# Attention in two query groups, the first pair of tiles routed during the second; one tile's activations gathered and led through the gates into the dense v

## The chip, the cores and the metric

The kernel runs on one core of one Trainium2 chip. The metric is the device time of one execution in microseconds (us). The kernel before takes 4099.25 us, the median of two runs (4098.07 and 4100.43). "TensorE" is the matrix engine (PE in the rows, PEld its weight loads), VectorE is DVE, ScalarE is ACT, GpSimd is POOL, and SP issues most of the DMAs.

## The reference, cut to what matters

Two layers over 512 latent and 256 context tokens. Layer 0 mixes with a state-space scan, layer 1 with attention (8 heads, keys for all 768 tokens, queries for the 512 latent ones). Each is followed by PEER: every token picks, in each of 8 heads, 16 of 16384 experts, and sums the experts' rows:

```python
idx, gate = peer_route(t, w_q, keys)             # 128 experts for each token
act = gelu(einsum('td,tkd->tk', h, u_tab[idx])) * gate
out = einsum('tk,tkd->td', act, v_tab[idx])
```

In layer 1 only the latent tokens are left: four tiles of 128 tokens, numbered 2 to 5.

## The kernel before, in words

A tile's PEER can be computed in two ways. **Gathered:** GpSimd fetches, by an indirect DMA, for each of 128 picks one u row for each token (a tile `row`, 128x1024 f32, 512 KB), VectorE multiplies it with the tile's input and sums it into one column of `act`; after gelu and the gate, 128 v rows are gathered and added up on VectorE (`gather`, lines 1323, 1330 and 1335). Five such `row` buffers exist, which wq and some attention tiles share. **Dense:** TensorE multiplies all 16384 u rows, in 128 blocks, with the dense tiles' inputs `Hs` (`dense_u`, line 1111: 24 matmuls a block, for the high and low halves of the operands), gelu gives `ge`, which is multiplied with a dense matrix of gates `Gt`, split into A's halves, and multiplied with the blocks of v (line 1180: 18 matmuls of 512 columns a block for three tiles). The gate matrix of a tile is made out of its routing by `gate_matrix`: 16 steps of 8 tokens, one-hot rows `e` and `o` on VectorE and ScalarE, small products `g_ps` on TensorE, and a copy to HBM (`gm`), from where `Gt` is read once per 8 blocks.

Layer 1 before: tiles 4, 2 and 3 are dense, tile 5 is gathered. `mla` runs attention over all 512 queries, head by head: `project` makes a head's queries and keys (`qps`, `kp_mla`), `scores` does a head's scores for one tile of queries, `values` the product with v; VectorE takes maxima and normalizes in each of these 32 steps. When attention is done come the output product and LayerNorm of both pairs of tiles (`out_steps`, line 791), the modulation and the routing queries (`query_steps`, line 920), then the routing of each tile (`route`, a long row of small VectorE operations). While tiles are routed, `ahead` computes 48 of the 128 u blocks early and puts them into HBM (`ged`), and `gate_matrices` follows the routed tiles. `peer` runs the rest: `dense_held` goes through the 128 blocks (80 of them with u still to do) with the sums held in PSUM, and the gather of tile 5 beside it.

The order on each engine comes from `merge`: it draws steps from several streams, always from the one whose clock (the sum of the numbers that its steps yield) is least; streams under `side` may be left unfinished. An engine executes its instructions in the order that results. `peer` first merges the gate matrices and the early u blocks, with the gather as a side stream, and only then the held pass.

Of the kernel before, what the change touches and what calls it, by code (L numbers as in the profile page):

```python
# [21 lines left out]
KD = 8  # L22
# [23 lines left out]
KU, LH, KL, GQ = 2, 4, 2, 4  # L46
GA = 3
# [60 lines left out]
class Net:  # L108
# [28 lines left out]
    def spare(self, shape, name, dt=F32):  # L137
        return self.pool.tile(shape, dt, tag="spare", bufs=max(3, len(self.tiles)), name=name)
# [673 lines left out]
    def s5_layer(self, dense, gather):  # L812
# [39 lines left out]
        def memory_ctx(_):  # L852
# [5 lines left out]
                                        self.query_steps(0, (2, 3), lambda: self.Hall[:, :, :, 0:256]),  # L858
                                        self.query_steps(0, (4, 5), lambda: self.Hall[:, :, :, 256:512]))
# [12 lines left out]
    def peer_setup(self, l, dense, gather):  # L872
        self.keysT = self.t4([128, 8, 128], "keysT")
        self.load(self.keysT, self.a["peer_keysT"][l])
        self.tiles, self.gathered = dense, gather
        self.h1 = {}
        self.qT, self.m, self.gat, self.routed = {}, {}, {}, {}
        self.gm = self.dram.tile([16, 128, len(dense), 4, 8, 32], F32, name=f"gm{l}")

    def peer_memory(self, l):  # L880
        self.phase(f"peer{l}")
        self.Hall = self.big([128, 2, KD, T_LAT], "Hs", F32R)
        self.Hs = self.Hall[:, :, :, T_LAT - len(self.tiles) * 128:]

    def query_steps(self, l, pair, H):
# [7 lines left out]
        def modulate(i, ti):  # L893
            mT = st[i] = self.mod_transpose(self.h1[pair][i], l, s, 3)
            if ti in self.tiles:
# [36 lines left out]
    def route(self, ti):  # L932
# [3 lines left out]
        dense = ti in self.tiles  # L936
# [90 lines left out]
        V.scalar_tensor_tensor(out=idx, in0=ii[:, 0, :], scalar=128.0, in1=ii[:, 1, :], op0=ALU.mult, op1=ALU.add)  # L1027
        gk = self.c5([128, 128], "gk")
# [57 lines left out]
    def gate_matrices(self, n_tiles):  # L1086
# [15 lines left out]
    def dense_u(self, Us):  # L1102

        PE, S = self.nc.tensor, self.nc.scalar
        TD = len(self.tiles) * 128
# [11 lines left out]
    def ahead(self, l, blocks, n_tiles):  # L1117

        NT = len(self.tiles)
# [15 lines left out]
    def dense_held(self, l):  # L1135
# [4 lines left out]
        NT = len(self.tiles)  # L1140
        TD = NT * 128
# [8 lines left out]
        def prep_u(b):  # L1150
# [4 lines left out]
            if b in self.early:  # L1155
                ge = self.t2([128, TD], "ge")
# [4 lines left out]
        def work_u(b, x):  # L1161
            ge = x if b in self.early else self.dense_u(x)
            gv = ge.rearrange("p (d g t) -> p d g t", d=NT, g=4)
            V.tensor_tensor(out=gv, in0=gv, in1=Gt[b // SB][:, :, :, b % SB, :], op=ALU.mult)
# [143 lines left out]
    def gather(self, l, row_time):  # L1308
# [3 lines left out]
        for ti in self.gathered:  # L1312
# [77 lines left out]
    def mla(self, dense, gather):  # L1390
# [73 lines left out]
        W = self.big([128, 12288], "mla_w")  # L1464
        wuq = W[:, 0:4608].rearrange("p (k n) -> p k n", k=3)
        wuqs = W[:, 4608:6144].rearrange("p (k n) -> p k n", k=3)
        wukv = W[:, 6144:10240].rearrange("p (k n) -> p k n", k=2)
        cosT, sinT = W[:, 10240:10752], W[:, 10752:11264]
# [3 lines left out]
        for k in range(2):  # L1472
            self.load(wukv[:, k, :], a["mla_w_ukv"][k * 128:(k + 1) * 128, :])
# [3 lines left out]
        wv = wukv.rearrange("p k (h x d) -> p k h x d", h=8, x=2)  # L1477
        for ti in range(6):
            for hf in range(2):
                vp = self.ps([128, 4, 128], "vp")  # L1480
                for k in range(2):
                    PE.matmul(out=vp, lhsT=ckvT[k][:, ti * 128:(ti + 1) * 128], rhs=wv[:, k, hf * 4:(hf + 1) * 4, 1, :],
                              start=(k == 0), stop=(k == 1))
                S.copy(out=v[ti][:, hf * 512:(hf + 1) * 512].rearrange("p (h d) -> p h d", h=4), in_=vp)
        oT, heads = [], {}

        def project(h):
            if h % 2 == 0:
                oT.append(self.t4([128, 2, T_LAT], "oT"))
                rp, rs = self.ps([128, 512], "rp"), self.ps([128, 512], "rs")  # L1490
                for k in range(3):
                    PE.matmul(out=rp, lhsT=wuq[:, k, 1024 + h * 64:1024 + (h + 2) * 64], rhs=cqT[k], start=(k == 0), stop=(k == 2))
                for k in range(3):
                    PE.matmul(out=rs, lhsT=wuqs[:, k, h * 64:(h + 2) * 64], rhs=cqT[k], start=(k == 0), stop=(k == 2))
                qr, qt = self.t2([128, T_LAT], "qr"), self.t2([128, T_LAT], "qt")
                V.tensor_tensor(out=qr, in0=rp, in1=cosT, op=ALU.mult)
                V.tensor_tensor(out=qt, in0=rs, in1=sinT, op=ALU.mult)
                V.tensor_tensor(out=qr, in0=qr, in1=qt, op=ALU.add)

                qs = self.row([128, 2, T_LAT], "qs", F32R)  # L1500
                for x in range(2):
                    r, o = slice(64 * x, 64 * x + 64), slice(64 - 64 * x, 128 - 64 * x)
                    S.copy(out=qs[r, x], in_=qr[r])
                    V.tensor_tensor(out=qs[o, x], in0=qr[r], in1=qs[r, x].bitcast(F32), op=ALU.subtract)
            else:
                qs = heads[h - 1][1]
            qnT = self.row([128, 2, T_LAT], "qnT", F32R)
            qps = self.ps([128, 512], "qps")
            for k in range(3):
                PE.matmul(out=qps, lhsT=wuq[:, k, h * 128:(h + 1) * 128], rhs=cqT[k], start=(k == 0), stop=(k == 2))  # L1510
            self.split(qnT[:, 0], qnT[:, 1], qps, V)
            kn = [self.t4([128, T], "knT", F32R) for _ in range(2)]
            for c0, n in ((0, 512), (512, 256)):
                kp = self.ps([128, 512], "kp_mla")
                for k in range(2):
                    PE.matmul(out=kp[:, 0:n], lhsT=wukv[:, k, h * 256:h * 256 + 128], rhs=ckvT[k][:, c0:c0 + n],
                              start=(k == 0), stop=(k == 1))
# [149 lines left out]
```

## Time and profile before

| | |
|---|---|
| median of the runs | 4099.25 us |
| the profiled execution | 4107.66 us, span of its instructions 4105.9 us |
| TensorE busy, mean granted clock | 91% of the span, 0.956 |
| VectorE, ScalarE, GpSimd busy | 75%, 35%, 30% |
| line 1111 (dense u), both layers | 1187.4 us with the high half of u, 759.6 us with the low half |
| DMA | 986 MB, 240 GB/s over the span |

Layer 1 begins at about 2334 us. Its attention runs from 2470 to 2686 us, the output product and the queries to 2806, routing with early u blocks to about 2955, gate matrices to 3182, the held pass from 3207 to 4087, and the last LayerNorms to 4106. A row of a window gives each engine's busy time in that stretch with the number of its instructions in brackets, then the granted clock, the share of the DMA engines' time and GB/s. In a timeline a row has start, length, engine, line and what is written and read; starts of successive matmuls lie closer than their lengths, since they are pipelined.

### The profile page before, as it was taken

What the parts mean: (1) busy time and instruction counts of PE and PEld (TensorE: products, weight loads), DVE (VectorE), ACT (ScalarE), POOL (GpSimd) and SP (SyncE); (2) the same over time, 40 slices, a digit from 0 to 9 for tenths busy, and PEclk for the clock granted to TensorE, in tenths of its full rate; (3) what the DMA queues carried; (4) which work ended last, traced back from release to release, by engine and by line L of the source; (5) the groups of instructions that cost most, each with busy time, mean ns of one, the idle gap of its engine ahead of it and who ended that gap; (6) DMA issues with size and microseconds to landing.
All of it is one profiled execution on the core that took longest, in us unless ns stands there. A gap on an engine that the chain in (4) does not pass through costs nothing.

```text
span 4105.9 us, 52738 instructions
## 1 busy us (share of the span) xinstructions
PE 3719.0 (91%) x18955; PEld 3031.4 (74%) x18955; DVE 3068.7 (75%) x6143; ACT 1450.2 (35%) x2527; POOL 1238.6 (30%) x940
## 2 busy tenths in 40 slices
PE   6759999888689999999999989998887899999998
PEld 3537768677667878778888855568887788888887
DVE  9784387976867788888898844438977677777764
ACT  1321123366632232232332243323466333333332
POOL 5743000022412455556555300000011344444410
PEclk7879999899999999999999999999999999999999
DMA  5457234377888899999999820144477889888873
GB/s 182 134 176 247 80 131 152 96 241 249 293 311 290 291 338 352 337 354 330 342 338 346 301 98 3 44 169 140 123 234 247 317 327 334 318 320 321 328 271 102
DMA packets 380007, 986.06 MB, mean 240 GB/s; under 512 B 64992, under 2 KB 145376, under 8 KB 375136
## 3 DMA queue, kind: packets, MB, share of 16 engines
q1 hardware_dynamic: 198688, 501.34, 35.4%
q0 software_dynamic: 110592, 402.70, 27.4%
q10 hardware_dynamic: 70464, 78.65, 5.5%
q8 instruction: 149, 2.44, 0.2%
q14 instruction: 114, 0.93, 0.1%
HBM read 892.28 MB, written 90.21 MB: 239 GB/s over the span
## 4 chain that ended last, share of the span: by engine, by line
PE 57%; DVE 14%; issue 12%; DMA 7%; POOL 6%; ACT 3%; SPq 0%; POOLq 0%; ACTq 0%; DVEq 0%
PE s_ps L1111 20%; PE acc L1180 8%; PE acc L1255 8%; POOL row L1323 5%; PE qp L920 3%; PE op L791 3%; DMA U<-in_peer_uT 3%; DMA row<-in_peer_v,idx 2%; PE g_ps L1076 2%; PE zp L762 2%; DVE Ul L306 1%; PE op_mla L1560 1%; DVE w L645 1%; PE yp L697 1%; DMA row<-in_peer_u,idx 1%
## 5 line engine op out<-in xcount | busy, mean ns | idle before, releaser
L1111 PE MATMUL s_ps<-Hs,Uh 128*128 128x512 f32 (+1 forms) x4096 | 1187.4, 371 | 13.5 <-ACT Uh L305 13.5
L1323 POOL DMA_INDIRECT row<-in_peer_u,idx x384 | 528.8, 1377 | 2025.2 <-DVE row L1330 1148.2
L1111 PEld LDWEIGHTS s_ps<-Hs,Uh 128*128 128x128 f32 x4096 | 763.1, 190 | 116.2 <-ACT Uh L305 18.7
L1111 PE MATMUL s_ps<-Hs,Ul 128*128 128x512 f32 (+1 forms) x2048 | 759.6, 371 | 27.2 <-DVE Ul L306 27.1
L1255 PE MATMUL acc<-Ws,A 128*128 128x512 f32 x2976 | 689.1, 393 | 37.5 <-ACT A L305 21.4
L1255 PEld LDWEIGHTS acc<-Ws,A 128*128 128x128 f32 x2976 | 564.3, 190 | 160.6 <-ACT A L305 21.9
L1323 POOL DMA_INDIRECT row<-in_peer_v,idx x384 | 502.9, 1310 | 516.8 <-DVE f L1335 460.7
L306 DVE TENSOR_TENSOR Ul<-U,Uh 128x1024 fp32r<-128x1024 f32 x256 | 312.0, 1219 | 281.8 <-ACT Uh L305 273.6
L1335 DVE SCALAR_TENSOR_TENSOR f<-row,act,f 128x1024 f32<-128x1024 f32 x381 | 487.1, 1278 | 33.8 <-DMA row<-in_peer_v,idx 32.2
L1330 DVE SCALAR_TENSOR_TENSOR row<-row,m 128x1024 f32<-128x1024 f32 x384 | 461.0, 1218 | 42.7 <-DMA row<-in_peer_u,idx 41.7
L1111 PEld LDWEIGHTS s_ps<-Hs,Ul 128*128 128x128 f32 x2048 | 389.5, 190 | 82.3 <-DVE Ul L306 35.3
L305 ACT CAST Uh<-U 128x1024 fp32r<-128x1024 f32 x256 | 268.0, 1050 | 500.0 <-DMA U<-in_peer_uT 454.4
L1180 PE MATMUL acc<-Wh,A 128*128 128x512 f32 x1536 | 426.6, 391 | 12.2 <-ACT A L305 12.2
L1076 PE MATMUL g_ps<-o,o 128*128 128x128 f32 x1792 | 240.3, 293 | 114.5 <-ACT o L1059 72.1
L1180 PEld LDWEIGHTS acc<-Wh,A 128*128 128x128 f32 x1536 | 288.3, 188 | 66.7 <-ACT A L305 12.6
L1114 ACT ACTIVATE ge<-s_ps 128x512 f32<-128x512 f32 (+1 forms) x256 | 138.8, 543 | 556.4 <-PE s_ps L1111 551.1
L1076 PEld LDWEIGHTS g_ps<-o,o 128*128 128x128 f32 x1792 | 229.7, 206 | 126.2 <-ACT o L1059 124.5
L305 ACT CAST A<-ge 128x512 fp32r<-128x512 f32 (+1 forms) x256 | 144.6, 565 | 309.0 <-DVE ge L1236 227.1
L305 ACT CAST Ws<-W 128x512 fp32r<-128x512 f32 x256 | 152.1, 619 | 264.3 <-DMA W<-in_peer_v 217.7
L1180 PE MATMUL acc<-Wl,A 128*128 128x512 f32 x768 | 237.5, 390 | 0.0
L306 DVE TENSOR_TENSOR Ws<-W,Ws 128x512 fp32r<-128x512 f32 x256 | 174.3, 684 | 56.0 <-ACT Ws L305 55.7
L306 DVE TENSOR_TENSOR A<-ge,A 128x512 fp32r<-128x512 f32 (+1 forms) x256 | 158.5, 620 | 54.2 <-ACT A L305 53.7
(340 smaller groups left out, 4780.3 us busy)
## 6 DMA issues: line engine op xcount, KB each, us to landing
U<-in_peer_uT SPq DMA_DIRECT2D x256, 512.0 KB
W<-in_peer_v SPq DMA_DIRECT2D x256, 256.0 KB
W<-in_peer_v SPq DMA_DIRECT2D x128, 512.0 KB
gm<-stage ACTq DMA_DIRECT2D x28, 2048.0 KB
ada_wt<-in_ada_w SPq DMA_DIRECT2D x96, 512.0 KB
Gt<-gm SPq DMA_DIRECT2D x16, 2048.0 KB
Gt<-gm SPq DMA_DIRECT2D x16, 1536.0 KB
wq<-in_peer_w_q SPq DMA_DIRECT2D x40, 512.0 KB
```

What stands on the lines that cost most here:

```text
L305: self.nc.scalar.copy(out=hi, in_=x)
L306: lo_eng.tensor_tensor(out=lo, in0=x, in1=hi.bitcast(F32), op=ALU.subtract)
L791: nc.tensor.matmul(out=op, lhsT=y(i, k), rhs=W, start=(k == 0), stop=(k == KD - 1))
L920: PE.matmul(out=st["p"][:, h % 2, i * 128:(i + 1) * 128], lhsT=W[:, k, :], rhs=st[i][:, k, :], start=(k == 0), stop=(k == KD - 1))
L1076: PE.matmul(out=gp[:, t, :], lhsT=o[1][:, t4 * 4 + t, :], rhs=o[0][:, t4 * 4 + t, :], start=True, stop=True)
L1111: PE.matmul(out=sp, lhsT=x[:, k, :], rhs=self.Hs[:, y, k, :], start=(n == 0), stop=(n == 3 * KD - 1))
L1114: S.activation(out=ge, in_=sp, func=AF.Gelu)
L1180: PE.matmul(out=acc[d][hf], lhsT=A[b][:, x, c], rhs=Ws[y][:, hf * 512:(hf + 1) * 512], start=(b == 0 and n == 0), stop=(b == NB - 1 and n ...
L1255: PE.matmul(out=acc[hf][d], lhsT=A[b][:, x, c], rhs=Ws[:, y], start=(j == 0 and n == 0), stop=(j == SB - 1 and n == 2))
L1323: GP.indirect_dma_start(out=r, out_offset=None, in_=tab, in_offset=bass.IndirectOffsetOnAxis(ap=ik[:, k:k + 1], axis=0), element_offset=l ...
L1330: x = V.scalar_tensor_tensor(out=r, in0=r, scalar=1.0, in1=m, op0=ALU.mult, op1=ALU.mult, accum_out=act[:, k:k + 1])
L1335: x = V.scalar_tensor_tensor(out=f, in0=r, scalar=act[:, k:k + 1], in1=f, op0=ALU.mult, op1=ALU.add)
```

## The change

Layer 1 alone is changed. Tile 4 stays among the dense tiles (it has a gate matrix and takes part in the product with v), but its u side is gathered: `gather` fetches its 128 u rows, forms gelu and the gate, and writes the result into the tile's routing record in place of the gates, so that the "gate matrix" of tile 4 holds finished activations. So `Hs`, `ge` and the dense u pass cover two tiles (256 columns) and not three (384); tile 4's third of A is split straight from `Gt`. The gather does tile 4 first, then tile 5 as before (u and v). `gate_matrices` does tiles 2 and 3, then tile 4, for which it waits until the gather of its u rows is done.

Attention runs in two groups of two query tiles: first tiles 4 and 5, then 2 and 3. Each group projects the queries of its own 256 tokens and, anew, the keys of all 768. `project` of the next head is issued behind the first scores of a head. During the second group the side streams do the output product, the LayerNorm, the queries and the routing of tiles 4 and 5, and begin the gather of tile 4. Output product, queries and routing of tiles 2 and 3, and the early u blocks, follow when attention is over.

```diff
-        for ti in self.tiles:
+        for ti in self.utiles + list(self.half):
             while ti not in self.routed:
                 yield 1.0
             yield from self.gate_matrix(ti)
...
-            self.split(A[b][:, 0], A[b][:, 1], ge, V)
-            return 0.0 if b in self.early else 5.2 * NT / 4
+            if TG:
+                hi, lo = (A[b][:, x, 0:TG].rearrange("p (d g t) -> p d g t", g=4, t=32) for x in range(2))
+                self.split(hi, lo, G[:, 0:NT - NU], V)
+            self.split(A[b][:, 0, TG:], A[b][:, 1, TG:], ge, V)
+            return 0.0 if b in self.early else 5.2 * NU / 4
...
             for ph, tab in ((0, a["peer_u"]), (1, a["peer_v"])):
+                if ph and ti in self.half:
+                    break
...
-                    V.tensor_tensor(out=act, in0=act, in1=gk, op=ALU.mult)
+                    V.tensor_tensor(out=gk if ti in self.half else act, in0=act, in1=gk, op=ALU.mult)
+            if ti in self.half:
+                self.routed[ti] = self.rts[ti]
+                continue
...
-        drain(pipeline([(lambda h=h, qi=qi: scores(h, qi), lambda pe, h=h, qi=qi: values(h, qi, pe))
-                        for h in range(8) for qi in range(4)], 2))
...
+        def attend(pair):
+            return pipeline([(lambda h=h, qi=qi: scores(pair, h, qi), lambda pe, h=h, qi=qi: values(pair, h, qi, pe))
+                             for h in range(8) for qi in range(2)], 2)
...
-        steps = out(p) + o1[:E1] + m0 + o1[E1:] + q0[:E2] + m1 + q0[E2:] + q1
+        drain(attend(p))
...
+        first = chain(pipeline(out(p) + m0 + q0, LT), *(self.route(ti) for ti in p))
+        merge(attend(q), side=(first, self.gathering))
+        while len(self.qT) < 2:
+            next(first)
...
+        steps = [(lambda: None, memory)] + out(q) + m1 + q1
         self.aheads = self.ahead(1, [b for b in range(128) if b % 8 < A1], 4)
-        self.gates = self.gate_matrices(4)
-        merge(scaled(pipeline(steps, LT), FA), chain(*(self.route(ti) for ti in order)), side=(self.aheads, scaled(self.gates, FG1)))
+        self.gates = self.gate_matrices(2)
+        merge(scaled(pipeline(steps, LT), FA), chain(first, *(self.route(ti) for ti in q)),
+              side=(self.aheads, scaled(self.gates, FG1), self.gathering))
...
-        self.mla([4, 2, 3], [5])
+        self.mla([4, 2, 3], [4, 5], [4])
```

Where the attention ends, TensorE's order before goes from the last product with v to both output products, into which the transposes of the first pair (`mt_ps`, which need its LayerNorm) and then the queries `qp` are mixed:

```order
4299 L1560 MATMUL op_mla<-pT,v 128x512 x6
4300 L791 MATMUL op<-wo,oT 128x512 x52
4301 L296 MATMUL mt_ps<-ident,h 128x128 x8
4302 L791 MATMUL op<-wo,oT 128x512
4303 L904 MATMUL m_ps<-ident,mT 128x128 x4
4304 L791 MATMUL op<-wo,oT 128x512
4305 L904 MATMUL m_ps<-ident,mT 128x128 x4
4306 L296 MATMUL mt_ps<-ident,h 128x128 x8
4307 L791 MATMUL op<-wo,oT 128x512 x10
4308 L920 MATMUL qp<-mT,wq 128x128 x80
4309 L296 MATMUL mt_ps<-ident,h 128x128 x16
4310 L920 MATMUL qp<-mT,wq 128x128 x48
```

At the same place TensorE now has, behind the last product with v of the second group:

```order
4357 L1584 MATMUL op_mla<-pT,v 128x256 x6
4358 L287 MATMUL tp_ps<-ident,pe 128x128 x12
4359 L1584 MATMUL op_mla<-pT,v 128x256 x6
4360 L792 MATMUL op<-wo,oT 128x512 x32
4361 L297 MATMUL mt_ps<-ident,h 128x128 x16
4362 L923 MATMUL qp<-mT,wq 128x128 x128
4363 L961 MATMUL sp<-keysT,qT 128x128 x8
4364 L1118 MATMUL s_ps<-Hs,Uh 128x256 x2
```

The first pair's work has moved ahead, between the steps of the second group; for the second pair the output product, the transposes and the queries stand one behind the other.

Before the held pass, VectorE's order now has the last steps of tile 3's gate matrix (`e`, `o`), the last split of an early u block (`Ul`), then the rest of tile 4's gathered u rows and the gate matrix of tile 4:

```order
3990 L1061 TENSOR_TENSOR e<-iota_68,iT 128x2048
3991 L1069 TENSOR_TENSOR o_24250<-e,gT 128x768
3992 L1343 SCALAR_TENSOR_TENSOR row,act<-row,m 128x1024
3993 L307 TENSOR_TENSOR Ul<-U,Uh 128x1024
3994 L1343 SCALAR_TENSOR_TENSOR row,act<-row,m 128x1024 x62
3995 L1355 TENSOR_TENSOR rt<-act,rt 128x128
3996 L1343 SCALAR_TENSOR_TENSOR row,act<-row,m 128x1024
3997 L1061 TENSOR_TENSOR e<-iota_68,iT 128x2048
3998 L1069 TENSOR_TENSOR o_24546<-e,gT 128x768
```

TensorE has at that place the last early block but three (`s_ps`), the last products of tile 3's gate matrix, and then the transposes of tile 4's record (`tr_ps`), which read what the 62 rows lead to:

```order
5128 L1118 MATMUL s_ps<-Hs,Uh 128x256 x2
5129 L1118 MATMUL s_ps<-Hs,Ul 128x256
5130 L1083 MATMUL g_ps<-o_24192,o_24190 128x128 x8
5131 L1083 MATMUL g_ps<-o_24250,o_24248 128x128 x8
5132 L1047 MATMUL tr_ps<-ident,rt 128x128 x3
5133 L1083 MATMUL g_ps<-o_24546,o_24544 128x128 x8
5134 L1083 MATMUL g_ps<-o_24554,o_24552 128x128 x8
```

Nothing of this stands in the order before: there the gate matrices follow one another between early u blocks.

## Rows read from the trace of the kernel before

**Rows 1.** Windows: PE, PEld, DVE, ACT, POOL busy us, clock, DMA share, GB/s.
```profile
2470.00:2686.00 216.00, 207.46 (x758) 117.64 (x757) 101.50 (x274) 84.03 (x226) 0.00 (x0) 0.98 0.10 37
2686.00:2806.00 120.00, 119.98 (x715) 88.11 (x714) 58.75 (x242) 29.21 (x65) 0.00 (x0) 1.00 0.48 159
2806.00:2955.00 149.00, 124.83 (x715) 118.17 (x714) 139.66 (x607) 65.45 (x101) 4.70 (x5) 0.91 0.42 134
2955.00:3207.00 252.00, 199.88 (x1313) 195.87 (x1311) 181.28 (x320) 153.40 (x272) 43.22 (x32) 0.94 0.72 240
3207.00:4087.00 880.00, 868.58 (x4224) 769.82 (x4224) 642.37 (x805) 304.14 (x421) 312.76 (x219) 1.00 0.82 296
...
1500.00:2300.00 800.00, 797.01 (x3461) 648.92 (x3460) 712.53 (x914) 242.33 (x368) 433.33 (x335) 1.00 0.94 341
```

**Rows 2.** Timeline of TensorE in the held pass, starts of three runs.
```profile
3500.29 0.63 PE L1180 MATMUL acc<-Wh,A 128*128 128x512 f32 x2
...
3504.39 0.51 PE L1111 MATMUL s_ps<-Hs,Uh 128*128 128x384 f32 x2
...
3507.55 0.52 PE L1111 MATMUL s_ps<-Hs,Uh 128*128 128x384 f32 x2
```

**Rows 3.** Timeline of TensorE in attention: 256 columns, and one head's keys.
```profile
2542.87 0.28 PE L1535 MATMUL sp_mla<-knT,qnT 128*128 128x256 f32 x1
2542.99 0.28 PE L1536 MATMUL sp_mla<-knT,qnT 128*128 128x256 f32 x1
...
2546.93 2.74 PE L1516 MATMUL kp_mla<-ckvT,mla_w 128*128 128x512 f32 x8
2549.48 0.50 PE L1534 MATMUL sp_mla<-knT,qnT 128*128 128x512 f32 x1
```

**Rows 4.** Groups by line and shape: count, busy us, mean ns, idle before.
```profile
L920 PE MATMUL qp<-mT,wq 128*128 128x128 f32 x1280 | 145.1, 275 | 0.0
...
L1054 DVE TENSOR_TENSOR e<-iota,iT 128x2048 bf16<-128x2048 bf16 x112 | 136.4, 1218 | 0.7 <-ACT iT L1044 0.7
...
L1062 DVE TENSOR_TENSOR o<-e,gT 128x768 f32<-128x768 bf16 x112 | 107.2, 957 | 9.6 <-DVE e L1054 0.5
```

**Rows 5.** Windows, VectorE alone, first of tile rw, then of tile oh.
```profile
2750.00:2990.00 240.00, 123.02 (x832) 0.94 0.45 143
2750.00:2990.00 240.00, 29.86 (x48) 0.94 0.45 143
```

**Rows 6.** Timeline of GpSimd: gathered rows, with DMA traffic beside them.
```profile
1802.44 1.45 POOL L1323 DMA_INDIRECT row<-in_peer_u,idx  x1 [0.31 <-issue]
1804.19 1.44 POOL L1323 DMA_INDIRECT row<-in_peer_u,idx  x1 [0.30 <-issue]
```

**Rows 7.** Timeline of GpSimd: the first gathered rows of layer 1.
```profile
2824.30 0.94 POOL L1323 DMA_INDIRECT row<-in_peer_u,idx  x1 [497.57 <-PE s_ps L1111]
2825.54 0.94 POOL L1323 DMA_INDIRECT row<-in_peer_u,idx  x1 [0.30 <-issue]
```

**Rows 8.** Timeline of VectorE: two gathered rows one behind the other.
```profile
1798.96 1.22 DVE L1330 SCALAR_TENSOR_TENSOR row<-row,m 128x1024 f32<-128x1024 f32 x1
...
1800.10 1.22 DVE L1330 SCALAR_TENSOR_TENSOR row<-row,m 128x1024 f32<-128x1024 f32 x1
```

**Rows 9.** DMA from 3550 to 3900 us: packets, MB, share of the engines; issues.
```profile
q0 software_dynamic: 15496, 56.43, 43.3%
...
row<-in_peer_v,idx POOLq DMA_INDIRECT x108
```

**Rows 10.** Timeline of TensorE from the last gate products to the held pass.
```profile
3180.49 2.05 PE L1076 MATMUL g_ps<-o,o 128*128 128x128 f32 x16 [1.62 <-ACT o L1059]
...
3207.45 1.22 PE L1180 MATMUL acc<-Wh,A 128*128 128x512 f32 x2 [12.23 <-ACT A L305]
```

**Rows 11.** Timeline of VectorE: LayerNorm of the second pair, first and last operation.
```profile
2743.73 0.69 DVE L797 TENSOR_TENSOR res<-op,m 128x512 f32<-128x512 f32 x1 [2.88 <-PE op L791]
...
2754.49 2.35 DVE L268 TENSOR_TENSOR h<-h,lnb 128x1024 f32<-128x1024 f32 x2
```

More of the change, by code (lines that the diff above doesn't have):

```diff
@@ L935, in route @@
         V, S, PE, GP = nc.vector, nc.scalar, nc.tensor, nc.gpsimd
-        dense = ti in self.tiles
+        dense = ti in self.utiles
         while ti not in self.qT:
@@ L1117, in ahead @@
     def ahead(self, l, blocks, n_tiles):
[L1119 removed]
+        NT = len(self.utiles)
         n = len(blocks)
@@ L1387, in dense_out, with mla @@
         return self.peer_out(l, ti, f, self.rows)
-    def mla(self, dense, gather):
+    def mla(self, dense, gather, half):
         nc, a = self.nc, self.a
@@ L1481, in mla @@
                 for k in range(2):
-                    PE.matmul(out=vp, lhsT=ckvT[k][:, ti * 128:(ti + 1) * 128], rhs=wv[:, k, hf * 4:(hf + 1) * 4, 1, :],
+                    PE.matmul(out=vp, lhsT=ckvT[k][:, ti * 128:(ti + 1) * 128], rhs=wv[k][:, hf * 4:(hf + 1) * 4, :],
                               start=(k == 0), stop=(k == 1))
                 S.copy(out=v[ti][:, hf * 512:(hf + 1) * 512].rearrange("p (h d) -> p h d", h=4), in_=vp)
-        oT, heads = [], {}
-        def project(h):
-            if h % 2 == 0:
[L1489 to L1500, printed above, removed]
@@ new lines, in mla, with project @@
+        oT, heads = {}, {}
+        kq, pTs = self.t16([128, 2, 2 * T + 512], "kq", F32R), self.t16([128, 2, 6, 256], "pT")
+        def project(pair, h):
+            q0 = (min(pair) - 2) * 128
+            tq = slice(q0, q0 + 256)
+            if h % 4 == 0:
+                oT.setdefault(pair, []).append(self.t4([128, 4, 256], "oT"))
+            if h % 2 == 0:
+                rp = self.ps([128, 2, 256], "rp")
+                for x, w in ((0, wuq[:, :, 1024 + h * 64:1024 + (h + 2) * 64]), (1, wuqs[:, :, h * 64:(h + 2) * 64])):
+                    for k in range(3):
+                        PE.matmul(out=rp[:, x], lhsT=w[:, k], rhs=cqT[k][:, tq], start=(k == 0), stop=(k == 2))
+                qr = self.t2([128, 2, 256], "qr")
+                V.tensor_tensor(out=qr[:, 0], in0=rp[:, 0], in1=cosT[:, tq], op=ALU.mult)
+                V.tensor_tensor(out=qr[:, 1], in0=rp[:, 1], in1=sinT[:, tq], op=ALU.mult)
+                V.tensor_tensor(out=qr[:, 0], in0=qr[:, 0], in1=qr[:, 1], op=ALU.add)
+                qs = self.row([128, 2, 256], "qs", F32R)
@@ L1511, in project @@
             self.split(qnT[:, 0], qnT[:, 1], qps, V)
-            kn = [self.t4([128, T], "knT", F32R) for _ in range(2)]
+            kn = kq[:, h % 2, 0:2 * T].rearrange("p (x t) -> p x t", x=2)
             for c0, n in ((0, 512), (512, 256)):
@@ L1551, in scores, with values @@
             V.tensor_scalar(out=pe, in0=pe, scalar1=rs_, scalar2=None, op0=ALU.mult)
-            return pe
-        def values(h, qi, pe):
-            pT = heads[h][3]
+            if qi == 0 and h < 7:
+                project(pair, h + 1)
+            return pe
+        def values(pair, h, qi, pe):
+            pT = heads[pair, h][3]
             self.transpose_to(pT[:, :, qi * 128:(qi + 1) * 128], pe, 6)
-            if qi == 3:
-                op = self.ps([128, 512], "op_mla")
+            if qi:
+                op = self.ps([128, 256], "op_mla")
@@ new lines, in out, with y @@
+        def out(pair):
+            def y(i, k):
+                c = (pair[i] - min(pair)) * 128
+                return oT[pair][k // 4][:, k % 4, c:c + 128]
+            return self.out_steps(1, pair, a["mla_w_o"], y, lambda ti: self.hd[ti], lambda: self.rows2)
+        p, q = tuple(gather), tuple(ti for ti in dense if ti not in half)
+        drain(attend(p))
+        self.peer_setup(1, dense, gather, half)
+        self.rows2 = rows(lambda shape, name: self.pool.tile(shape, F32, tag="rows", bufs=3, name=name))
```

107 lines of the change are left out of this document (56 added, 51 removed).

## The prediction

> **What bounds the kernel now.** I read layer 1 stretch by stretch, by the windows first: in each, the engine whose busy time fills the stretch sets its length. In attention TensorE is busy 207 of 216 us, in the output products and queries 120 of 120. In the routing stretch VectorE takes over, 140 of 149 us (94%). From there to the held pass nobody is full: TensorE 200 of 252, VectorE 181, ScalarE 153, a chain of the three. The held pass is TensorE's, 869 of 880 us, with the DMA engines at 0.82 and VectorE at 73% [rows 1]. So a cheaper dense u pays in full only in the held pass, and what is done before that pass pays or costs by whoever sets its stretch.
>
> **The dense u pass.** In the held pass 18 matmuls of 512 columns take 3504.39 - 3500.29 = 4.10 us, 0.228 each; the next 18 of 384 columns take 3.16 us, 0.176 each [rows 2]. 128 columns are worth 0.052 us, so I price 256 columns at 0.124. The bounds: matmuls of 256 columns in attention start 0.12 apart [rows 3], and 128x128 products that load new weights each time run at 145.1 us for 1280, 0.113 each [rows 4], so the weight loads allow it; at worst it stays at 0.176. The Trainium skill speaks against this change here ("TensorE: Matmul & The Clock Gate", "What overlaps and what doesn't"): a weight load overlaps a running matmul only where the row groups differ. By it load and matmul would add up in these full-height matmuls, and little of a narrower matmul would be gained below the load's own time. The trace disagrees, since the 0.113 above holds load and product together.
>
> 80 blocks are left in the held pass: 80 x 24 x 0.052 = 100 us less TensorE work. The 48 early blocks save 60 us of TensorE, but in a stretch where VectorE will be the longer one, so I count nothing for them.
>
> **The held pass.** 880 us become 880 - 100 = 780. The other engines there: VectorE loses a third of the width of `ge` and A and gains 128 small splits, about even; gathered rows go from 219 [rows 1] to 242 by the new order. A row costs the DMA engines 0.433 x 350 us / 108 = 1.40 us [rows 9], so they have 0.82 x 880 + 23 x 1.40 = 754 us of work, less some 9 for smaller `ged`: 745 of 780, 0.955. Layer 0's pass runs at 0.94 with TensorE 100% busy and VectorE at 89% [rows 1], so I allow only 3 us: 783.
>
> **Attention.** Keys are projected twice. One head's keys take 2549.48 - 2546.93 = 2.55 us of TensorE [rows 3], 8 heads 20 us. Half of 216 + 20 is 118; moving `project` ahead of its use may save a little: 116 for the first group. The second group has the other half and also the first pair's output product and queries, half of the 120 us. By the order, 9 of its 16 steps and these 60 us stand before the first routing operation: 66 + 60 = 126 us of TensorE. Of the remaining 7 steps VectorE is the longer: attention's 101.5 us over 32 steps, and the doubled key splits (some 9 us), are 3.45 a step, 24; routing costs (123.0 + 29.9) / 4 = 38, with unlisted small operations 40 a tile [rows 5], of which tile 4 and two thirds of tile 5 lie here, 66; 10 gathered rows at 1.14 [rows 8], 11. That is 101 us, and at the 94% of the routing stretch 108. Attention ends at 2470 + 116 + 126 + 108 = 2820, where before it was 2686.
>
> **The second pair.** Its chain is bare now: output product 29 us, LayerNorm from 2743.73 to 2756.84, 13 us [rows 11], during which TensorE has nothing else (before, queries lay beneath it), some 5 for transposes and modulation, queries 30. These 77 us end at 2897; before it was 2806.
>
> **Routing, early blocks, gate matrices of tiles 2 and 3.** VectorE's work up to the run of 62 rows: two tiles routed 80, 47 splits `Ul` as long as a gathered row (54), 40 gathered rows (46), 32 pairs `e` and `o` at 1.22 + 0.96 less overlap (67) [rows 4]: 247 us. TensorE has about 195. The routing stretch before kept VectorE at 94%, the stretch of gates at 72% [rows 1]; nearer to the first, since routing runs through most of it, 0.895 gives 276 us, ending at 3173 (bounds 260 and 305).
>
> **The run of 62 rows.** Of tile 4's 128 rows 66 lie before this point. The gate matrix of tile 4 waits for all, VectorE's `e` and `o` for it are queued behind them, and TensorE's next instruction is the transpose of that record: TensorE stands idle. A row cannot go faster than VectorE's 1.14 us [rows 8], GpSimd's issue every 1.24 when nothing else runs [rows 7], or the 1.40 of DMA time; beside heavy traffic the issue takes 1.75 [rows 6]. I take 1.5, near the DMA time since little else moves: 93 us, to 3266 (bounds 77 and 108). The Trainium skill's fit for such DMAs ("DMA: Bandwidth & Descriptors", "Anatomy of one DMA") is 2.0 us plus the bytes over 436 GB/s, an estimate of 3.2 us for 512 KB; with four rows in flight that leaves the issue as the limit, and the run would be 77 us. No run here shows four rows in flight undisturbed.
>
> Tile 4's gate matrix follows with nothing beside it: VectorE 16 x 2.1 + 14 rows x 1.14 = 50 us, a start of 5, gaps: 60, to 3326. From the last gate product to the held pass it is 3182.5 to 3207.4, 25 us (the copy to HBM and back) [rows 10]. The held pass starts at 3351, 144 us later than before.
>
> **The sum.** 3351 + 783 = 4134. The end was 19 us; now about 10 gathered rows stand behind the last A, and a fourth tile has its LayerNorm there: 29, to 4163. The span before was 4105.9 in an execution of 4107.66, and the median of the runs is 4099.25; taking off 6.7 gives 4156 us. About 100 us of the change's gain and 10 of its loss lie at the end, 144 of loss ahead: +57, or 1.4%.
>
> **Rivals.**
> *The row ring sets the run (slower).* If a row's way from issue to use, with five buffers, costs what layer 0's rows took beside its dense pass, 800 us / 335 = 2.39 us a row [rows 1], the run takes 148 us: 4211. For it: the issue waits for VectorE's release. Against: there the pace was set by how the two streams are mixed. Above 1.9 us a row the change is slower by over 2%.
> *The DMA engines set the held pass (slower).* If they cannot hold more than the 0.89 or so of its busiest part, 745 / 0.89 = 837: 4210. Against it stand layer 0's 0.94.
> *The front hides better.* Routing inside attention costs only what TensorE needs (7 steps, 52 us, and 56 saved), the stretch of routing and gates runs at 94% (261), the run at 1.24: 4156 - 56 - 15 - 16 = 4069. Against it: VectorE's order is fixed, and its work there is longer than TensorE's.
> *The change doesn't do what it says:* weight loads keep 256 columns at 0.176: 4256. The 0.113 speaks against it.
>
> **How the numbers follow.** A difference under 2% (82 us, so 4017 to 4181) is about what a measurement of this kernel cannot tell from no change. My forecast has 0.50, of which 0.12 lie above 4181 by its own bounds (each of three terms can grow by 15 to 30 us); the ring 0.13; the DMA engines 0.12; the hidden front 0.20, of which 0.04 below 4017 with the held pass at its best as well; the weight loads 0.03; the rest, 0.02, within 2%. That makes faster 0.04, same 0.56, slower 0.40. The range of the likeliest is 4110 to 4195; to hold 8 in 10 it takes in most of the ring, the DMA engines and the hidden front: 4075 to 4225.
>
> **What would show it.** In the profile after: matmuls of line 1118 with 256 columns 0.12 apart; an end of attention near 2820 with VectorE full in its last 100 us; a gap of TensorE of 90 us or more, in which VectorE runs line 1343 alone; the first `acc` near 3350; and then some 783 us to the last. A first `acc` before 3260 or a held pass of over 820 us would make the prediction wrong.

## The result, and the profile after

The changed kernel takes 4229.49 us (median of 2 runs, 4227.76 to 4231.21) against 4099.25: 1.032 times as long, 95% interval 1.027 to 1.036. It is slower by more than 2%, and 4.5 us above the predicted range. The profiled execution has a span of 4225.9 us.

These are windows of the changed kernel, with the columns of [rows 1]. The stretches are: first query group; second group with the first pair's output products and queries; second group with routing; second pair's output products and queries; routing and early blocks; gate matrices of tiles 2 and 3 and early blocks; rows alone; tile 4's gate matrix; held pass; tail.

```profile
2462.00:2581.00 119.00, 115.08 (x513) 83.62 (x512) 59.44 (x164) 47.13 (x129) 0.00 (x0) 1.00 0.06 21
2581.00:2705.00 124.00, 111.41 (x537) 78.78 (x536) 44.18 (x112) 37.71 (x94) 0.00 (x0) 0.94 0.23 71
2705.00:2813.00 108.00, 79.05 (x373) 58.27 (x373) 95.42 (x511) 28.00 (x74) 13.47 (x13) 0.79 0.27 88
2813.00:2896.00 83.00, 64.69 (x340) 47.83 (x339) 48.37 (x98) 14.11 (x31) 20.08 (x18) 0.88 0.78 272
2896.00:3046.00 150.00, 101.94 (x707) 95.43 (x705) 136.47 (x516) 59.08 (x93) 25.21 (x20) 0.84 0.54 172
3046.00:3223.00 177.00, 133.11 (x958) 127.74 (x957) 106.42 (x121) 103.60 (x182) 24.68 (x20) 0.89 0.69 222
3223.00:3327.00 104.00, 0.00 (x0) 0.00 (x0) 76.10 (x125) 0.31 (x1) 75.76 (x60) 0.51 0.90 316
3327.00:3399.00 72.00, 42.94 (x329) 39.97 (x329) 53.41 (x66) 46.51 (x90) 24.32 (x16) 0.88 0.87 307
3399.00:4187.00 788.00, 769.72 (x4224) 671.72 (x4224) 633.54 (x941) 301.06 (x545) 340.62 (x237) 0.98 0.90 331
4187.00:4226.00 39.00, 0.00 (x0) 0.00 (x0) 31.07 (x59) 5.67 (x8) 0.78 (x1) 0.55 0.42 156
```

The held pass fell from 880 [rows 1] to 788 us, as wanted. It begins 192 us later (3399 against 3207), and 20 us more stand behind it. In the line of 3223 TensorE does nothing for 104 us. In the line of 3046 no engine is full: TensorE 0.75, VectorE 0.60, ScalarE 0.59.

| step of the prediction | predicted, us | measured, us |
|---|---|---|
| attention ends | 2820 | 2813 |
| second pair's queries end | 2897 | 2896 |
| stretch up to the run of rows | 276 | 327 |
| run of rows | 93 | 104 |
| tile 4's gate matrix, to the first `acc` | 85 | 72 |
| held pass | 783 | 788 |
| tail | 29 | 39 |
| median of the runs less the profiled span | -6.7 | +3.6 |

### The profile page after: what moved, and what is told of

It is laid out like the page before. It is cut to its first block, busy times and chain, and to the rows that moved or that the text cites. A ratio compares the mean times of both kernels' runs of the same rounds, so it can differ in the third digit from the quotient of the medians.

```text
span 4225.9 us, 54297 instructions
## 1 busy us (share of the span) xinstructions
PE 3612.5 (85%) x19219; PEld 2943.3 (70%) x19219; DVE 3215.5 (76%) x6580; ACT 1453.9 (34%) x2685; POOL 1400.3 (33%) x1068
## 4 chain that ended last, share of the span: by engine, by line
PE 45%; DVE 19%; issue 17%; DMA 9%; POOL 6%; ACT 2%; SPq 1%; DVEq 0%; POOLq 0%; ACTq 0%
PE s_ps L1118 13%; PE acc L1266 10%; DMA U<-in_peer_uT 5%; POOL row L1336 5%; PE acc L1191 4%; PE qp L923 3%; PE op L792 2%; PE zp L763 2%; DVE row L1343 2%; DVE f L1348 1%; DVE Ul L307 1%; DMA row<-in_peer_v,idx 1%; DVE rw L953 1%; DVE tk_tmp L951 1%; DVE w L646 1%
## 5 line engine op out<-in xcount | busy, mean ns | idle before, releaser
L1336 POOL DMA_INDIRECT row<-in_peer_u,idx x512 | 678.0, 1324 | 2131.1 <-DVE row L1343 1162.2
L1118 PE MATMUL s_ps<-Hs,Uh 128*128 128x512 f32 (+1 forms) x4096 | 1052.3, 347 | 48.6 <-ACT Uh L306 48.3
L1118 PEld LDWEIGHTS s_ps<-Hs,Uh 128*128 128x128 f32 x4096 | 729.6, 196 | 152.4 <-ACT Uh L306 55.1
L1118 PE MATMUL s_ps<-Hs,Ul 128*128 128x512 f32 (+1 forms) x2048 | 714.9, 349 | 43.6 <-DVE Ul L307 43.6
L1336 POOL DMA_INDIRECT row<-in_peer_v,idx x384 | 516.5, 1345 | 510.3 <-DVE f L1348 450.9
L1343 DVE SCALAR_TENSOR_TENSOR row<-row,m 128x1024 f32<-128x1024 f32 x512 | 615.7, 1218 | 77.8 <-DMA row<-in_peer_u,idx 75.2
L1118 PEld LDWEIGHTS s_ps<-Hs,Ul 128*128 128x128 f32 x2048 | 401.0, 196 | 98.7 <-DVE Ul L307 51.9
L1121 ACT ACTIVATE ge<-s_ps 128x512 f32<-128x512 f32 (+1 forms) x256 | 125.1, 489 | 422.0 <-PE s_ps L1118 416.7
L306 ACT CAST A<-ge 128x512 fp32r<-128x512 f32 (+1 forms) x256 | 130.6, 512 | 296.2 <-DVE ge L1247 218.2
L1191 PEld LDWEIGHTS acc<-Wl,A 128*128 128x128 f32 x768 | 144.6, 188 | 31.7
```

Of the source, the lines that this page charges most:

```text
L306: self.nc.scalar.copy(out=hi, in_=x)
L1118: PE.matmul(out=sp, lhsT=x[:, k, :], rhs=self.Hs[:, y, k, :], start=(n == 0), stop=(n == 3 * KD - 1))
L1121: S.activation(out=ge, in_=sp, func=AF.Gelu)
L1191: PE.matmul(out=acc[d][hf], lhsT=A[b][:, x, c], rhs=Ws[y][:, hf * 512:(hf + 1) * 512], start=(b == 0 and n == 0), stop=(b == NB - 1 and n ...
L1336: GP.indirect_dma_start(out=r, out_offset=None, in_=tab, in_offset=bass.IndirectOffsetOnAxis(ap=ik[:, k:k + 1], axis=0), element_offset=l ...
L1343: x = V.scalar_tensor_tensor(out=r, in0=r, scalar=1.0, in1=m, op0=ALU.mult, op1=ALU.mult, accum_out=act[:, k:k + 1])
```

## The experiments

Times are medians of 4 runs, ratios with 95% intervals are to the kernel before on the same chip (4098 to 4102 us). "After" is the changed kernel, 4229 us, a median of two runs. Windows are of one profiled execution each. Layer 0, which only `before_ul2` changes, ends in them between 2356 and 2365 us, so that places in layer 1 can lie up to 10 us apart without any cause in the edit; lengths of stretches are the safer measure.

### What each part costs: split_only, serial

Both drain the two query groups one behind the other and put the output products, queries and routing behind them, in the order of the kernel before; this edit they share. `split_only` keeps tile 4 dense; `serial` gathers its u side ("half gathering" below).

```diff
         drain(attend(p))
+        drain(attend(q))
...
-        merge(attend(q), side=(first, self.gathering))
...
-        self.mla([4, 2, 3], [4, 5], [4])
+        self.mla([4, 2, 3], [5], [])
```

The last pair of lines is in `split_only` alone.

> From the kernel before, the attention alone is cut in two query groups of 256 columns, drained one after the other; tile 4 stays wholly dense, the first pair is routed where it was. The keys of eight heads are projected twice. If the cut costs what the first group alone took in the changed kernel (119 us, so 238 for two against 216 before): about 22 us, 4121 us in all. If the doubled projections lie under VectorE's and ScalarE's work: no change, 4099 us.

Measured: 4119.74 us, ratio 1.005 (1.003 to 1.007). From its first `qps` to its last product with v attention takes 236 us (2462 to 2698), 20 more than before (216, from 2471).

> The changed kernel without its overlap: both query groups are drained before the first pair's output projection, queries and routing, tile 4 half gathered as in the changed kernel. Theory A (the overlap pays): the routing of two tiles and the queries come back after the attention, and the time is 4260 us or more, 30 or more above the changed kernel's 4229. Theory B (VectorE's work only moved): the attention ends at 2697 instead of 2813, last queries about 2817 instead of 2896, and the stretch behind it is the old 376 us plus 50 for rows and the run's 102: about 4200 us, faster than the changed kernel, so the overlap itself would cost time.

Measured: 4194.72 us, 1.023 (1.021 to 1.025): theory B. Windows of `serial`: routing and early blocks, gate matrices of tiles 2 and 3, rows alone.

```profile
2817.00:3045.00 228.00, 163.97 (x1157) 153.76 (x1156) 215.91 (x823) 89.82 (x138) 38.22 (x34) 0.88 0.64 200
3045.00:3157.00 112.00, 78.01 (x545) 73.09 (x543) 88.11 (x106) 77.99 (x146) 30.23 (x20) 0.86 0.69 229
3157.00:3289.00 132.00, 0.00 (x0) 0.00 (x0) 95.58 (x156) 0.36 (x2) 101.67 (x78) 0.51 0.90 320
```

So the change's 130 us, with its parts added in this order, are three losses: the split 20, the half gathering 75, the overlap 35, each uncertain by some 5 us. In the half gathering (`serial` against `split_only`) the held pass gives 90 us, but rows alone on the path and tile 4's gate matrix behind them take more. In the overlap (after against `serial`) attention up to the last queries takes 434 us instead of 352. From there to the end of the run, VectorE's work fell by 81 us (399.6, the sum of the three lines above, to 319.0), and the time by only 41 (472 to 431).

### What holds the stretch of 327 us: la3, early32, rows_late, ul_later

```diff
-  for i, b in enumerate(blocks)], LA)
+  for i, b in enumerate(blocks)], LA + l)
```

> The changed kernel with the early blocks of layer 1 prepared three steps ahead instead of two, so that the ScalarE split of the next block stands ahead of the copies of g_ps in ScalarE's queue. Theory of the chain (ScalarE, TensorE and VectorE take turns in 2896 to 3223): that stretch of 327 us shortens by 20 to 60 us, 4170 to 4210 us in all. Theory of VectorE's work (its instructions are what fills the stretch): no change, 4221 to 4237 us. Theory of late rows (the gathered rows hold VectorE up): no change either.

Measured: 4237.34 us, 1.034 (1.032 to 1.036). The stretch is 327 us again. One step more of lead only moved TensorE's wait, from `Uh` to `o`. Waits from 3050 to 3220, in the changed kernel and in `la3` (engine, line, what was waited for, us in total, times, longest):

```profile
PE s_ps L1118 <- ACT Uh L306: 23.1, 12, 4.2
```

```profile
PE g_ps L1083 <- ACT o L1066: 39.9, 12, 8.8
```

The first of these waits is 2.2 us in `la3`, and the second 4.3 in the changed kernel.

```diff
-A0, A1 = 40, 3
+A0, A1 = 40, 2
```

> The changed kernel with 32 early blocks instead of 48; the 16 others go through the held pass, where each costs 24 products of 256 columns, 24 x 0.123 = 2.95 us, 47 us in all. In 2896 to 3223 they are gone. If ScalarE, TensorE and VectorE take turns there (177 us for some 25 blocks and 32 gate steps behind the routing): 60 to 95 us less, 4180 to 4215 us. If TensorE's own time is what counts: 47 us less, 4229 us. If VectorE's work sets the stretch: 16 x 1.23 = 20 us less, 4256 us.

Measured: 4213.02 us, 1.027 (1.025 to 1.029). Windows of `early32`: gate matrices of tiles 2 and 3, and the held pass.

```profile
3052.00:3163.00 111.00, 79.84 (x573) 75.32 (x573) 87.59 (x105) 80.07 (x150) 30.96 (x20) 0.91 0.76 253
...
3342.00:4192.00 850.00, 817.03 (x4584) 714.01 (x4583) 669.92 (x979) 323.93 (x576) 339.95 (x237) 0.98 0.87 319
```

With 16 blocks fewer in it the stretch of gate matrices is 66 us shorter (177 to 111), 4.1 us a block. TensorE's busy time fell by 3.3 us a block and VectorE's by 1.2: more came back than either engine's own work, and nearly the sum of the two. That speaks for the theory of turns. The total says less than the stretch. It lies in that theory's range, but the held pass begins 57 us earlier and takes 62 us longer, so that the 16 us won are about what the tail became shorter, 18.

```diff
-                    return row_time
+                    return RH if ti in self.half and ph == 0 else row_time
+RH = 9.0
```

> The changed kernel, but the order gives each of tile 4's u rows a step of 9.0 instead of 3.0: about 22 of them instead of 66 stand ahead of the run, and the run grows by about 44. If a row ahead of 3046 costs VectorE's whole 1.15 to 1.3 us (VectorE is busy 0.93 there): 31 rows fewer give back 36 to 40 us, the run takes 44 x 1.66 = 73 more, 4262 to 4266 us in all. If idle time took the rows there: nothing comes back, 4302 us. In 3046 to 3223 the 13 rows fewer change the length by 15 us if VectorE's work sets it, by nothing if ScalarE and TensorE take turns.

Measured: 4282.85 us, 1.045 (1.043 to 1.047), between the two theories. 105 rows now stand alone, and take 1.68 us each. 43 rows fewer stand ahead of them, and the run begins 20 us earlier (3203), 0.47 a row (0.58 counted from the end of layer 0). VectorE's idle time carried more than half of their 1.3 us. Behind the routing, 13 rows fewer gave 7 us.

The order itself shows the turns. This is the timeline of the changed kernel in one turn, with idle time and what ended it in brackets.

```profile
3072.83 0.38 ACT L1121 ACTIVATE ge<-s_ps 128x256 f32<-128x256 f32 x1 [0.65 <-PE s_ps L1118]
3073.50 0.59 ACT L1085 COPY stage<-g_ps 128x512 f32<-128x512 f32 x1 [0.28 <-PE g_ps L1083]
...
3074.53 1.04 ACT L306 CAST Uh<-U 128x1024 fp32r<-128x1024 f32 x1 [0.45 <-ACT stage L1085]
...
3075.61 1.23 DVE L307 TENSOR_TENSOR Ul<-U,Uh 128x1024 fp32r<-128x1024 f32 x1 [4.04 <-ACT Uh L306]
3076.75 1.22 DVE L1061 TENSOR_TENSOR e<-iota,iT 128x2048 bf16<-128x2048 bf16 x1
3078.01 1.05 ACT L1066 CAST o<-e 128x1024 f32<-128x1024 bf16 x1 [1.45 <-DVE e L1061]
...
3079.61 1.95 PE L1083 MATMUL g_ps<-o,o 128*128 128x128 f32 x16
```

Read it as a ring. ScalarE's `Uh` stands in its queue behind `ge` and `stage`, which wait for TensorE. VectorE's `Ul` waits 4.04 us for `Uh`. The next one-hots `e` stand behind `Ul` on VectorE, `o` behind `e`, and TensorE's gate products behind `o`. `ul_later` cuts the ring at one place: `Ul` is put one step behind `Uh`, so that the next `e` isn't behind a wait.

```diff
+            for j in range(n + 2):
+                if j < n:
+                    hi[j] = high(blocks[j])            # load U, ScalarE: Uh
+                if 0 <= j - 1 < n:
+                    lo[j - 1] = low(*hi.pop(j - 1))    # VectorE: Ul
+                if j >= 2:
+                    yield work(j - 2, lo.pop(j - 2))
```

> The changed kernel; in layer 1's early blocks VectorE's low part of a block is put one step behind ScalarE's high part in the order, so that VectorE no longer stands waiting for ScalarE (65 us of such waits in 3050 to 3220) ahead of the next one-hots. Theory of taking turns through the queues: the stretch from 3046 to 3223 shortens by 25 to 60 us, 4170 to 4204 in all. If the wait only moves to another engine, as with one step more of lead: 4229 us.

Measured: 4192.14 us, 1.022 (1.020 to 1.024). The waits from 3046 to 3223 in the changed kernel, and then those of `ul_later` in the same stretch (3049 to 3190).

```profile
DVE Ul L307 <- ACT Uh L306: 67.8, 21, 6.0
ACT o L1066 <- DVE e L1061: 32.5, 18, 3.6
```

```profile
ACT ge L1121 <- PE s_ps L1118: 29.2, 18, 3.9
DVE Ul L1146 <- ACT Uh L1141: 27.7, 12, 6.3
```

VectorE's wait fell from 67.8 to 27.7 us, and `o`'s wait for `e` no longer is among the first seven. From the end of the routing to the run it takes 144 us where it took 177. Window of that stretch in `ul_later`:

```profile
3049.00:3193.00 144.00, 120.28 (x975) 117.75 (x973) 108.33 (x124) 99.44 (x181) 29.44 (x22) 0.96 0.82 272
```

TensorE's clock is part of the gain. Beside the line of 3046 above, TensorE is busy 120 us instead of 133 for about as many products, at a granted clock of 0.96 instead of 0.89. In the changed kernel 320 of 503 successive products of the early blocks start 0.12 us apart and 135 some 0.21; in `ul_later` it is 429 and 63 of 523. Of those 135, 103 lie where the profile has the clock at 1.2 GHz instead of 2.4, and of the 320 none. So about 13 of the 33 us are TensorE's own work done faster. No run holds the clock fixed, so how much the waits alone cost stays open.

The same edit in `serial`:

> The later low part (as in the run before, 4192 us on the changed kernel) in the kernel that drains both query groups before the routing (4195 us without it). There VectorE is 0.88 busy in 2817 to 3181, so less can be won: if the overlap's loss is the stretch that did not shrink, 10 to 15 us, about 4183, and with-overlap and without come within 10 us of each other. If the overlap loses elsewhere: 37 us here as well, 4158 us.

Measured: 4183.18 us, 1.021 (1.019 to 1.023), 11.5 less than `serial`. With this ring cut, the kernel with the overlap is 9 us above the one without, where it was 35: by these runs most of the overlap's loss was the stretch that had become bound by turns.

### What the rows cost: rows_early, short_rows, tail27

`rows_early` is the edit of `rows_late` with RH = 1.5.

> The changed kernel, but the order gives each of tile 4's u rows a step of 1.5 instead of 3.0, so that all 128 are placed ahead of the last early blocks: 64 of them before the first early block, and no run of 62 rows is left. If VectorE's idle time takes them (2705 to 2896 has 191 us with 144 busy): the run's 102 us go, 64 x 1.15 = 74 us of row work come into 47 us of idle time, +27, so about 75 us less: 4155 us. If rows placed there delay the routing and the attention one for one (each 1.15 or more): about 30 us less, 4200 us. If the rows' transfers bind (1.66 us each wherever they stand): no gain, 4229 us.

Measured: 4196.71 us, 1.024 (1.022 to 1.026): 33 less, the middle case. 92 rows stand ahead of the end of the routing instead of 46, which moves from 3046 to 3101: 55 us for 46 rows, 1.2 a row. Beyond the first 46, VectorE's idle time takes almost none. The held pass begins 45 us earlier (3354) but takes 801 us instead of 788, for which no run shows a cause.

```diff
-  x = V.scalar_tensor_tensor(out=r, in0=r, scalar=1.0, in1=m, ...)
+  w = 64 if ti in self.half else D
+  x = V.scalar_tensor_tensor(out=r[:, 0:w], in0=r[:, 0:w], scalar=1.0, in1=m[:, 0:w], ...)
```

> The changed kernel with the product of each of tile 4's u rows cut to 64 of 1024 columns (the rest of the inner product is left out; the rows are still fetched whole): VectorE's 1.31 us a row falls to about 0.2. Theory of the issue (in the run a row issue of GpSimd that starts while a VectorE instruction runs lasts as long as that instruction's rest plus 0.81 us, one that starts free 0.94): all issues fall to 0.94, a row in the run takes 0.94 + 0.30 = 1.24 us, the run 62 x 1.24 = 77 us instead of 102. Theory of the transfers (512 KB a row at the 316 GB/s of the run, DMA share 0.90): 1.5 us a row or more, the run 93 us or more. Ahead of 3046, where VectorE is busy 0.93, 47 rows x 1.1 = 52 us come back in either; 4152 by the first, 4165 to 4177 by the second.

Measured: 4180.72 us, 1.020 (1.018 to 1.023). The run takes 84 us, 1.35 a row. Timeline of the run in the changed kernel, GpSimd's issues and VectorE's products:

```profile
3258.20 1.90 POOL L1336 DMA_INDIRECT row<-in_peer_u,idx  x1 [0.30 <-issue]
3259.33 1.23 DVE L1343 SCALAR_TENSOR_TENSOR row<-row,m 128x1024 f32<-128x1024 f32 x1
3260.41 0.96 POOL L1336 DMA_INDIRECT row<-in_peer_u,idx  x1 [0.30 <-issue]
...
3261.22 1.23 DVE L1343 SCALAR_TENSOR_TENSOR row<-row,m 128x1024 f32<-128x1024 f32 x1 [0.65 <-DMA row<-in_peer_u,idx]
3261.67 1.58 POOL L1336 DMA_INDIRECT row<-in_peer_u,idx  x1 [0.30 <-issue]
```

The issue at 3261.67 starts 0.78 us ahead of the end of VectorE's product (3262.45) and takes 0.78 + 0.80 us. With short products, in the run of `short_rows`, and the window of that run:

```profile
3231.02 0.94 POOL L1336 DMA_INDIRECT row<-in_peer_u,idx  x1 [0.34 <-issue]
3231.63 0.23 DVE L1344 SCALAR_TENSOR_TENSOR row<-row,m 128x64 f32<-128x64 f32 x1 [1.05 <-DMA row<-in_peer_u,idx]
...
3232.30 0.94 POOL L1336 DMA_INDIRECT row<-in_peer_u,idx  x1 [0.34 <-issue]
```

```profile
3192.00:3276.00 84.00, 0.37 (x1) 0.18 (x1) 14.64 (x127) 0.31 (x1) 56.23 (x60) 0.52 1.01 394
```

All 60 issues take 0.93 to 0.97 us, one each 1.28 in the lines shown, though the DMA engines are fuller (share 1.01 against 0.90, 394 GB/s against 316). So it isn't the traffic that made issues slow in the run, but VectorE's running product. The theory of the transfers, 93 us or more, falls. 50 of the 60 issues start 0.30 to 0.4 us behind the last, waiting for nothing that the profile shows; the other ten wait 12 us in all for a row to be used, which is why it is 84 and not 77 us. The run begins 31 us earlier, where 52 were expected, so the total lies above both forecasts; as in `rows_late`, part of the row work had lain in idle time.

```diff
-                    return row_time
+                    return RL if l and ti not in self.half else row_time
+RL = 2.75
```

> The changed kernel, but the order gives each row of the last gathered tile a step of 2.75 instead of 3.0, so that its rows and its LayerNorm end ahead of the last held products. If the tail of 39 us is the gather that came late: it falls to about 25 us, 4215 us in all. If the rows moved ahead cost the held pass as much (VectorE 634 of 787 busy, DMA share 0.90): no change, 4229 us.

Measured: 4241.35 us, 1.034 (1.031 to 1.036), no gain. Windows of `tail27`: held pass and tail.

```profile
3399.00:4218.00 819.00, 782.76 (x4221) 679.15 (x4221) 648.54 (x964) 303.87 (x546) 339.03 (x236) 0.97 0.88 323
4218.00:4238.00 20.00, 0.86 (x4) 0.38 (x2) 15.34 (x35) 4.11 (x6) 0.00 (x0) 0.65 0.20 79
```

The tail became 19 us shorter and the held pass 31 longer. The rows moved ahead had no free place there.

### Can early blocks fill the run: early112, serial112, before112

In the changed kernel, in `serial` and in the kernel before:

```diff
-A0, A1 = 40, 3
+A0, A1 = 40, 7
```

> The changed kernel with 112 early blocks instead of 48, so that early blocks are left to stand between the rows of the run (order there: 2.6 for a block, 3.0 for a row). Theory of the uncovered run (the change loses because 62 rows and tile 4's gate matrix have nothing beside them on TensorE): the 64 blocks more take 64 x 3.2 to 4.4 us where they stand, less the run of 104, +100 to +180, and give back 64 x 3.9 = 250 us in the held pass (the price that 32 instead of 48 showed): 70 to 150 us less, 4080 to 4160. Theory of conserved work (rows, gate steps and blocks take turns there too, so that nothing is hidden): 64 x 4.4 = 280 come in, 250 go: 4229 to 4260 us.

Measured: 4266.90 us, 1.040 (1.039 to 1.042), above both forecasts.

> 112 early blocks in the kernel that drains both query groups before any routing and gathers half of tile 4 (4195 us with 48). If the uncovered run is what half gathering loses: 100 us or so less, about 4090 us, at the time of the kernel before or under it. If not: 4195 to 4225.

Measured: 4266.21 us, 1.040 (1.038 to 1.042), above both as well. TensorE still has a gap of 64 us here, where `serial` has 133, and the tail takes 135 us.

> The kernel before with 112 early blocks instead of 48: it has no run of rows, its TensorE is 0.83 busy in 2806 to 3182. If early blocks only gain by covering a run: no gain, 4100 us or above it (64 blocks x 384 columns cost in either place what TensorE takes). If they gain in themselves: 30 us or more less, and a gain of the two kernels above would show nothing about the run.

Measured: 4132.87 us, 1.007 (1.006 to 1.009). Windows of `early112`, held pass and tail:

```profile
3513.00:4131.00 618.00, 588.47 (x2686) 488.35 (x2687) 493.95 (x823) 218.81 (x417) 252.78 (x180) 0.97 0.90 336
4131.00:4267.00 136.00, 0.78 (x4) 0.32 (x2) 104.35 (x116) 5.66 (x8) 72.31 (x58) 0.51 0.75 263
```

The lone run is gone, and 64 blocks more cost only 114 us ahead of the held pass (it begins at 3513 instead of 3399). They give back 170 there. But the pass is now too short for tile 5's 256 rows: the last 58 are issued behind it, and the tail takes 136 us. Nor do early blocks gain in the kernel before. The theory of the uncovered run falls as an explanation of the whole loss: covering it moves it to the end.

### The same edit elsewhere: before_ul, before_ul2, rows_early_ul

The edit of `ul_later` in the kernel before, in layer 1 (`before_ul`) and in both layers (`before_ul2`), and in `rows_early`.

> The later low part in layer 1's early blocks of the kernel before. VectorE stands 48 us for ScalarE's high parts in 3006 to 3180 there. If that wait holds the gate stretch in the kernel before too: 15 to 40 us less, 4060 to 4085 us. If TensorE (0.83 to 0.87 busy there) has no more to give: 4100 us.

Measured: 4072.98 us, ratio 0.994 (0.992 to 0.996). Windows of the kernel before from the end of its routing to its last gate product (2989 to 3182), and of `before_ul` between the same two events (2978 to 3150):

```profile
2989.00:3182.00 193.00, 157.71 (x1057) 155.44 (x1058) 138.55 (x157) 130.35 (x237) 35.80 (x26) 0.94 0.75 246
```

```profile
2978.00:3150.00 172.00, 158.36 (x1085) 156.16 (x1086) 141.00 (x159) 130.79 (x238) 42.70 (x29) 0.96 0.85 283
```

TensorE's 158 us fill 0.92 of the stretch instead of 0.82. The ring stood in the kernel before as well.

> As the run above, with the same edit in layer 0's 40 early blocks too. If they have the same wait: a few us less again (5 to 30). If not: the same time as the run above.

Measured: 4042.22 us, 0.986 (0.985 to 0.988). This is 1.4% faster than the kernel before. Layer 0 ends at 2332 us, where all other runs have it at 2356 to 2365, and attention begins at 2443 instead of 2476, so layer 0's early blocks had the wait too.

> The later low part together with tile 4's u rows placed ahead of the early blocks (4197 us alone, VectorE 0.84 busy in 2936 to 3265). If the two gains add: 33 + 37 us, 4160 us. If VectorE is then full: 4175 us or above.

Measured: 4172.39 us, 1.018 (1.016 to 1.020). The two gains add to 57 of 70 us, between the two forecasts; every version that gathers half of tile 4 stays behind the kernel before.

## Why the prediction was wrong

**Dense u pass and held pass: right.** Matmuls of 256 columns start 0.12 us apart where the clock is full, as priced; the held pass took 788 for 783, with the DMA engines at 0.90. Timeline of TensorE in an early block:

```profile
3061.80 0.28 PE L1118 MATMUL s_ps<-Hs,Uh 128*128 128x256 f32 x1
3061.92 0.28 PE L1118 MATMUL s_ps<-Hs,Ul 128*128 128x256 f32 x1
3062.04 0.40 PE L1118 MATMUL s_ps<-Hs,Uh 128*128 128x256 f32 x2
```

**Attention and the second pair: right** within 7 us each, with VectorE at 95 of the last 108 us. The 7 us early are not the forecast's merit: from its first `qps` to its end attention took 354 us (2459 to 2813) for a forecast of 350, but it began 12 us earlier, 9 of them from layer 0, which the change leaves alone.

**Routing, early blocks, gate matrices: the step that failed, by 51 of the 73 us.** The work was right: VectorE's 247 us were 243. The quotient was wrong: one share of 0.895 for the whole stretch, "nearer to the first, since routing runs through most of it". Routing ran through 150 of the 327 us, with VectorE at 0.91. Behind it, in 177 us, VectorE was at 0.60, and no engine's work fills that stretch. `early32` (4.1 us a block) and `ul_later` (-37 us) show what lengthens it: the queues of ScalarE, VectorE and TensorE, each in its own order, wait for one another, at a granted clock of 0.89 where `ul_later` has 0.96. The rows held the sign already: by [rows 1] the stretch of gates ran at 0.72 in the kernel before, and with the measured division of the work, 136.5 / 0.94 + 106.4 / 0.72 is 293. Of the remaining 34 us 5 lie in the routing, at 0.91, and 29 behind it, from 0.72 down to 0.60. With `Ul` one step later VectorE is at 0.75 there (108 of 144 us). Why the ring cost more here than in the kernel before, which has it too, no run shows.

The same error stands in the overlap: 81 us of VectorE's work left the part behind attention, and 41 us of time, while attention became 82 us longer.

**The run: mechanism right, size off**, 1.68 for 1.5 us a row, +11 us, inside its bounds. I read the issue interval of 1.75 in [rows 6] as an effect of heavy traffic and so shortened it for a quiet stretch. It was VectorE's product running, which a run of rows alone keeps: in the kernel before, all 116 row issues that started with over 0.35 us of a u-row product left took that rest plus 0.81 us (within 0.12), against 0.94 for a free one [rows 7]. Nor were the 1.40 us of DMA time the floor that I took them for: in `short_rows` a row took 1.35, and most issues stood 1.28 apart.

**Tile 4's gate matrix** took 72 for 85, **the tail** 39 for 29; `tail27`, the one other order tried for it, did not save those 10 us. My correction from span to median (-6.7) was another 10 us: the profiled execution was slower than both runs before and is the faster of the two here (+3.6).

**The rivals.** The row ring and the DMA engines did not come: the run stayed under its 1.9 us a row, the held pass at 788. The hidden front did not either: it needed VectorE at 0.94 throughout. The loss came from the forecast's own middle, which the text bounded at 305 us and which took 327. My signs of being wrong asked for an early first `acc` (before 3260) or a long held pass; a late first `acc`, 3399 for 3350, was what came.

## What to carry to other kernels

Divide a stretch where its bound changes before turning work into time, and use each part's own busy share; work taken from a part where queues wait for one another gives back less than its own time, here about half (41 of 81 us). In such a part, look for an instruction that waits for another engine and has the next step's first instruction behind it: one step later in the order was worth 37 us here and, in both layers, 60 in the kernel before. An operation is cheap in another engine's idle time only while that lasts: 43 of the rows ahead of the run cost some 0.5 us each, 46 more cost 1.2, a lone one 1.68. Look at the granted clock of a stretch before you call TensorE's busy time its work: here 133 us at 0.89 were 120 at 0.96.

## What the hardware showed that I had not expected

A row issue on GpSimd that starts while VectorE works on two SBUF tensors waits for that instruction's end. In the kernel before, the changed one and `serial`, of the issues that met over 0.35 us of a 128x1024 u-row product, 415 of 424 took its rest plus 0.81 us, and nine took 0.94 as if free; for `e` it was 164 of 164. For the sum of v rows into `f` in the last two, 53 of 99 took the rest plus 0.81, 12 waited longer, and 34 took 0.94. The exceptions are near ties: the nine start within 0.03 us of VectorE's instruction and the 34 within 0.07, while every issue that waited starts later, by 0.04 us or more in the u rows and 0.14 or more under `f`. The Trainium skill has the rule ("SBUF — State Buffer", "Who interferes with whom"): a VectorE instruction with two SBUF inputs contends with a GpSimd instruction that reads SBUF, and the port pair that they share is an exclusive lock. The trace agrees, as far as starts so close together can tell who came first.
